# Attention's scores as split products, with the remainder of the keys as two row tiles

## The chip, the cores and the metric

The kernel runs on one core of a Trainium2 chip. The metric is the device time of one execution in microseconds (us), lower is better. The engines of the core run their own instruction streams in order and wait for one another by semaphores: TensorE (matmuls, and transposes as matmuls), VectorE (DVE in the rows), ScalarE (ACT), GpSimd (POOL), and SyncE (SP), whose queue issues most transfers (DMA).

## The reference

A model of two blocks works on 1024 tokens of width 1024 in float32. The first block has two layers; each mixes three branches, of which only the second one matters here: differential attention with 4 heads. Queries and keys of a head have two components of 64 features each, with rotary positions; values have 128 features.

```
q, k: (2 components, 4 heads, 1024 tokens, 64)       # after rope, q scaled by 1/8
for each block of 128 queries:
    s = einsum('cbhqd,cbhkd->cbhqk', qblk, k)         # both components
    p = softmax(s, axis=-1)
    w = p[0] - lam * p[1]
    o = einsum('bhqk,bhkv->bhqv', w, v)
o = rms_norm(o) * (1 - lambda_init);  output o * silu(g)
```

The other branches (gated linear scans), the output projection, and the second block (convolution, recurrent unit, 32 routed experts) are the rest of the time and are not edited.

## The kernel before, in words

Matmuls that need float32 accuracy are done in one of two ways. The projections split each operand into a float32r part and the float32r rest (`ATh` and `ATl` hold the normalized input so, features over partitions) and add three float32r products (`mm3`, L379 to L381). Attention's products are plain fp32 matmuls, which the hardware runs as two records for each instruction.

In each layer the projections of heads 0 and 1 (`dq0`, `dk0`, `dv0`) come first, among the scans. `rope` (L913 to L928) rotates a pair of 128-token tiles with VectorE and GpSimd, transposes them with TensorE into PSUM (`pT`), evacuates them with ScalarE (L925) into a tile `h` and stores it to the DRAM buffers `qd` and `kd` (L928). `values` (L933) stores v into `dvd`. Then comes the attention proper. Head 0 runs while the projections of heads 2 and 3 (`other_projections`: 24 steps, five behind each of the first periods) are still going; heads 1 to 3 run without them.

A head needs Q, K and v in SBUF. `head_prep` makes the list of its loads (L982 to L984). For head 0 they go to tiles of the pool `hp_` (`QS`, `KH`, `v`). For heads 1 to 3 they go into regions of `ATh` and `ATl`, the normalized input itself, so they must wait until the last projection has read that region: heads 1 and 3 take feature slices 6 and 7, head 2 takes slices 2 and 3. Both components lie side by side in the free dimension; the 64 features take 64 partitions. Q is loaded twice, into partitions 0 to 63 and 64 to 127; K's first 512 keys go to the lower partitions, the second 512 to the upper ones.

The work of attention is written as periods, one for each block of 128 queries, 8 for each head. A period does two half steps, one for each component. In a half step TensorE does the scores of the new block (`scores`, L1002: two matmuls of 64 rows, one for each half of the keys, on row tiles that lie side by side, into two PSUM banks `pS`), four transposes of the weights of a block two periods older (`turned`, L1034, `pW`), and two products with v of one still older (`weighted`, L1049, `pO`). VectorE takes the row maximum (L1005), ScalarE the exponential (L1007), VectorE joins the components (L1019 to L1022). Every four blocks `squared`, `summed` and `headnorm` (L1058 to L1072) normalize. `put` chains these calls on TensorE, VectorE and ScalarE, so their order on each of the engines is the written one. Everything else is placed by a planner that works from modelled times when the program is built: it picks what it takes for ready, in the order of the program's text. So a transfer that stands later in the text can be issued ahead of one that is not ready.

From `PRELOAD`, a head's loads are listed during the head before it (block 5 of head 0, block 2 of heads 1 and 2), three for each period. PSUM has two buffers for `pS`, three for `pW` and the projections, one for `pO`.

Of the kernel before, what the change touches and what calls it, by code (L numbers as in the profile page):

```python
# [11 lines left out]
F32 = mybir.dt.float32  # L12
# [215 lines left out]
def r32(ap):  # L228
    return ap.bitcast(F32)
# [7 lines left out]
def kernel(ctx: ExitStack, tc: tile.TileContext, A: dict, out: bass.AP, upto=99, dbg=None):  # L237
# [41 lines left out]

    qd = dr.tile([4, 64, 2, S], F32, name="qd")  # L280
    kd = dr.tile([4, 64, 2, S], F32, name="kd")
    dvd = dr.tile([4, 128, S], F32, name="dvd")
# [446 lines left out]
    for l in range(DEPTH):  # L729
# [170 lines left out]
        def place(at, shape, dt, **kw):  # L900
            if at[1] in ("st", "sh"):
                kw["bufs"] = 2
            return at[0].tile(shape, dt, tag=at[1], name="pl", **kw)

        def rope(n, hp, i, w, acc, tr, at, eng=G):
# [14 lines left out]
            for hh in range(2):  # L920
                for ii in range(2):
                    T.transpose(pT[:, hh, ii * 128:ii * 128 + 128],
                                asm[0][:, ii, hh * 4:hh * 4 + 4].rearrange("p b d -> p (b d)"), ident)
            h = place(at[2], [128, 2, 256], F32)
            rope.last = SC.activation(h, pT, AF.Copy, scale=0.125 if n == 0 else 1.0)  # L925
            dst = (qd, kd)[n][2 * hp:2 * hp + 2, :, :, (i - 1) * 128:(i + 1) * 128]
            for c in range(2):
                SY.dma_start(dst[:, :, c].rearrange("h x t -> x h t"), h[c * 64:c * 64 + 64])  # L928

# [6 lines left out]

        at1 = ((st, "q"), (st, "t2r"), (st, "sgb"))
        for n, nm in enumerate(("dq", "dk")):
# [27 lines left out]
        def head_prep(h):  # L966


            if h == 0:
                Q, K, v = (hp_.tile([128, n, 512], F32, tag=t, name=t) for t, n in (("QS", 4), ("KH", 2), ("v", 2)))  # L970
            else:
                a = 2 if h == 2 else 6
                Q, K, v = r32(ATh[:, a:a + 2]), r32(ATl[:, a]), r32(ATl[:, a + 1])
            if h == 0:
                Q = Q.rearrange("p (c k) t -> p c (k t)", c=2)
                v = v.rearrange("p k t -> p (k t)")
            else:
                K = K.rearrange("p (c t) -> p c t", c=2)
            loads = []
            for d_ in range(2):  # L980
                rows = slice(d_ * 64, d_ * 64 + 64)
                loads.append(lambda rows=rows: SY.dma_start(Q[rows], qd[h]))  # L982
                loads.append(lambda rows=rows, d_=d_: SY.dma_start(K[rows], kd[h, :, :, d_ * 512:d_ * 512 + 512]))
            loads.append(lambda: SY.dma_start(v, dvd[h]))  # L984
            return {"h": h, "ops": (Q, K, v.rearrange("p (k d) -> p k d", k=8)), "loads": loads}

# [8 lines left out]
        def scores(q, c):  # L995

            st, i, sm = q["st"], q["i"], q["sm"]
            Q, K = st["ops"][:2]
            p = sc_.tile([128, 2, 512], F32, tag="s", name="pS")
            for kc in range(2):  # L1000
                rows = slice(kc * 64, kc * 64 + 64)
                put("pe", lambda: T.matmul(p[:, kc, :], Q[rows, c, i * 128:(i + 1) * 128], K[rows, c, :],  # L1002
                                           start=True, stop=True))
            pf = p.rearrange("p a b -> p (a b)")
            put("dve", lambda: V.tensor_reduce(sm[:, c:c + 1], pf, axis=AX.X, op=OP.max, negate=True))  # L1005
            ec = aw.tile([128, S], F32, tag=f"e{c}", name=f"e{c}", bufs=3)
            put("act", lambda: SC.activation(ec, pf, AF.Exp, bias=sm[:, c:c + 1], accum_out=sm[:, 2 + c:3 + c]))  # L1007
            q["e"].append(ec)
# [90 lines left out]
        def other_projections():  # L1099
            got = {0: wq1}  # L1100
            at2 = ((hp_, "st"), (aw, "sg"), (hp_, "sh"))

# [1025 lines left out]
```

## Time and profile before

| | |
|---|---|
| median of 3 runs | 2889.11 us (2883.72 to 2891.49) |
| the profiled execution's own time | 2893.09 us |
| its span, first to last instruction | 2891.2 us |
| TensorE busy with matmuls | 2669.6 us (92%) |
| VectorE, ScalarE busy | 1712.3 us (59%), 1262.3 us (44%) |
| mean granted TensorE clock | 0.966 |

Busy shares are means over stages with different limits. The records of a matmul overlap their neighbours, so the time of a group on TensorE is best read from the start of one group to the start of the next. The granted clock is the share of full speed; it has two levels, 1.00 and 0.50.

### The profile page before, as it was taken

To read this page: it belongs to the slowest core of one execution; us is meant where nothing else is said; L and a number is where in the kernel's file an instruction comes from. 1 tells how busy PE (TensorE), PEld (TensorE's weight loads), DVE (VectorE), ACT (ScalarE), POOL (GpSimd) and SP (SyncE) were. 2 spreads that over 40 slices of the span, in tenths; PEclk is the share of its full clock that TensorE was granted. 3 is DMA by queue.
4 is the path that set the end of the run, shared out by engine and by line. 5 is a ranking of instruction groups with operands and counts; after the bars stand their busy time and mean duration, and the time that the engine had idled before them with its cause. 6 is when DMAs were issued, how large, how long until landed. Compare 5 with 4: busy or idle time off the path is not lost. (4 is left out here: it accounts for less than half of the span.)

```text
span 2891.2 us, 39821 instructions
## 1 busy us (share of the span) xinstructions
PE 2669.6 (92%) x15462; PEld 2087.7 (72%) x15462; DVE 1712.3 (59%) x2530; ACT 1262.3 (44%) x2078; POOL 722.4 (25%) x564
## 2 busy tenths in 40 slices
PE   7998998999999999989999999889799999999968
PEld 6887887755988878878558887679566666566558
DVE  6767663476357576633773493663655456455566
ACT  5343322366343424323663412642554445455545
POOL 1323131142214141311431342530211111121122
PEclk9999999999999999999999999989899999999979
DMA  4221223432322212233413323033688889799761
GB/s 152 66 79 62 88 88 79 102 102 63 128 85 73 79 64 94 83 80 81 111 63 132 109 75 106 30 119 124 272 338 344 328 306 392 298 360 377 312 265 71
DMA packets 140213, 446.78 MB, mean 155 GB/s; under 512 B 14432, under 2 KB 51360, under 8 KB 113760
## 3 DMA queue, kind: packets, MB, share of 16 engines
q1 hardware_dynamic: 131040, 412.26, 40.5%
q0 software_dynamic: 8960, 31.72, 3.1%
q8 instruction: 128, 2.10, 0.3%
q14 instruction: 85, 0.70, 0.1%
HBM read 367.25 MB, written 76.68 MB: 154 GB/s over the span
## 5 line engine op out<-in xcount | busy, mean ns | idle before, releaser
L379 PE MATMUL pK<-wh,ATh 128*128 128x256 f32 x1280 | 373.8, 293 | 24.3 <-DVEq L623 10.7
L1650 DVE TENSOR_TENSOR ews<-raw,ews 128x2048 fp32r<-128x2048 f32 x120 | 277.3, 2325 | 187.6 <-ACT ews L1649 185.8
L380 PE MATMUL pK<-wl,ATh 128*128 128x256 f32 x1280 | 370.5, 290 | 7.3 <-DVE wl L362 7.3
L381 PE MATMUL pK<-wh,ATl 128*128 128x256 f32 x1280 | 366.7, 288 | 1.8 <-POOL ATl L1414 1.8
L379 PE MATMUL pF<-ATh,wh 128*128 128x512 f32 (+1 forms) x800 | 321.4, 403 | 1.7 <-ACT g L1335 0.9
L380 PE MATMUL pF<-ATl,wh 128*128 128x512 f32 (+1 forms) x800 | 320.9, 401 | 0.3 <-DVE ATl L350 0.2
L381 PE MATMUL pF<-ATh,wl 128*128 128x512 f32 (+1 forms) x800 | 319.5, 400 | 0.1
L1649 ACT ACTIVATE ews<-raw 128x2048 fp32r<-128x2048 f32 x124 | 234.6, 1910 | 156.5 <-PE h L381 62.6
L379 PEld LDWEIGHTS pK<-wh,ATh 128*128 128x128 f32 x1280 | 249.2, 195 | 38.8 <-issue 16.1
L380 PEld LDWEIGHTS pK<-wl,ATh 128*128 128x128 f32 x1280 | 249.5, 195 | 14.3 <-DVE wl L362 8.1
L381 PEld LDWEIGHTS pK<-wh,ATl 128*128 128x128 f32 x1280 | 247.9, 194 | 5.5 <-issue 2.8
L1005 DVE TENSOR_REDUCE sm<-pS 128x1 f32<-128x1024 f32 x128 | 156.3, 1221 | 111.2 <-PE pS L1002 111.1
L1007 ACT ACTIVATE e<-pS,sm 128x1024 f32<-128x1024 f32 x128 | 142.4, 1113 | 170.3 <-DVE sm L1005 164.6
L379 PEld LDWEIGHTS pF<-ATh,wh 128*128 128x128 f32 (+1 forms) x800 | 150.1, 188 | 40.3 <-issue 4.0
L380 PEld LDWEIGHTS pF<-ATl,wh 128*128 128x128 f32 (+1 forms) x800 | 149.8, 187 | 38.4 <-issue 5.6
L379 PE MATMUL h<-ews,xh 128*128 128x512 f32 (+1 forms) x416 | 168.6, 410 | 9.3 <-ACT xh L1831 5.1
L381 PEld LDWEIGHTS pF<-ATh,wl 128*128 128x128 f32 (+1 forms) x800 | 149.9, 187 | 36.9 <-issue 4.3
L380 PE MATMUL h<-ews,xh 128*128 128x512 f32 (+1 forms) x416 | 168.5, 406 | 2.8 <-DVE ews L1650 2.8
L381 PE MATMUL h<-ews,xl 128*128 128x512 f32 (+1 forms) x416 | 168.0, 405 | 3.4 <-DVE xl L1833 3.4
L1848 POOL DMA_INDIRECT xb<-hfd,tab x38 | 53.2, 1399 | 456.1 <-PE pT L1830 447.6
L379 PE MATMUL pK<-wo,ATh 128*128 128x256 f32 x512 | 149.0, 291 | 9.7 <-ACT ATh L1195 9.7
L380 PE MATMUL pK<-wo,ATh 128*128 128x256 f32 x512 | 147.2, 288 | 0.0
(462 smaller groups left out, 6086.5 us busy)
## 6 DMA issues: line engine op xcount, KB each, us to landing
raw<-in_w_dram SPq DMA_DIRECT2D x192, 1024.0 KB, 11.1
ws<-in_wp_dram SPq DMA_DIRECT2D x64, 512.0 KB, 4.8
xd<-x SPq DMA_DIRECT2D x24, 512.0 KB, 2.6
x<-xd SPq DMA_DIRECT2D x17, 512.0 KB, 6.0
x<-in_x_dram SPq DMA_DIRECT2D x16, 512.0 KB
sgd<-sgb SPq DMA_DIRECT2D x32, 256.0 KB, 2.8
sg<-sgd SPq DMA_DIRECT2D x32, 256.0 KB
yd<-oT SPq DMA_DIRECT2D x32, 256.0 KB, 2.0
```

Source lines behind the costliest of these rows:

```text
L379: T.matmul(ps, ah, bh, start=first, stop=False)
L380: T.matmul(ps, ah, bl, start=False, stop=False)
L381: T.matmul(ps, al, bh, start=False, stop=last)
L1005: put("dve", lambda: V.tensor_reduce(sm[:, c:c + 1], pf, axis=AX.X, op=OP.max, negate=True))
L1007: put("act", lambda: SC.activation(ec, pf, AF.Exp, bias=sm[:, c:c + 1], accum_out=sm[:, 2 + c:3 + c]))
L1649: SC.activation(w[:, 0], s_, AF.Copy)
L1650: eng.tensor_tensor(w[:, 1], s_, r32(w[:, 0]), op=OP.subtract)
L1848: G.indirect_dma_start(out=xb[:n], out_offset=None, in_=hfd, in_offset=bass.IndirectOffsetOnAxis(ap=idx, axis=0))
```

## The change

`rope` now writes two tiles: `h`, the transposed tile rounded to float32r by ScalarE as before, and `lo`, the rest, which VectorE computes from `pT` and `h`; both are stored, so `qd` and `kd` get a dimension for the two parts. `lo` has one buffer.

The scores become three products: with Q the two parts of the queries, one below the other over 128 partitions, and K the keys' first part, twice, once below the other, one float32r matmul of 128 rows gives (first + rest of q) x (first part of k) for each half of the keys. Then a pair of 64-row matmuls adds the first part of q (Q2) times the rest of k (Kl). The product of the two rests is left out, as in the projections.

A head's loads go from 5 to 8: Q over all 128 partitions in one transfer, K twice with all 1024 keys, Q2 twice, Kl in two halves, v. Heads 1 and 3 now take slices 4 to 7 of `ATh` and `ATl`, head 2 slices 0 to 3.

```diff
-    qd = dr.tile([4, 64, 2, S], F32, name="qd")
-    kd = dr.tile([4, 64, 2, S], F32, name="kd")
+    qd = dr.tile([4, 2, 64, 2, S], F32, name="qd")
+    kd = dr.tile([4, 2, 64, 2, S], F32, name="kd")
...
-            h = place(at[2], [128, 2, 256], F32)
-            rope.last = SC.activation(h, pT, AF.Copy, scale=0.125 if n == 0 else 1.0)
-            dst = (qd, kd)[n][2 * hp:2 * hp + 2, :, :, (i - 1) * 128:(i + 1) * 128]
-            for c in range(2):
-                SY.dma_start(dst[:, :, c].rearrange("h x t -> x h t"), h[c * 64:c * 64 + 64])
+            h = place(at[2], [128, 2, 256], F32R)
+            lo = place(at[3], [128, 2, 256], F32R, bufs=at[3][2])
+            sc = 0.125 if n == 0 else 1.0
+            rope.last = SC.activation(h, pT, AF.Copy, scale=sc)
+            V.scalar_tensor_tensor(lo, pT, sc, r32(h), op0=OP.mult, op1=OP.subtract)
+            dst = (qd, kd)[n][2 * hp:2 * hp + 2, :, :, :, (i - 1) * 128:(i + 1) * 128]
+            for a, t in enumerate((h, lo)):
+                for c in range(2):
+                    SY.dma_start(dst[:, a, :, c].rearrange("h x t -> x h t"), r32(t[c * 64:c * 64 + 64]))
...
-                a = 2 if h == 2 else 6
-                Q, K, v = r32(ATh[:, a:a + 2]), r32(ATl[:, a]), r32(ATl[:, a + 1])
...
-            for d_ in range(2):
-                rows = slice(d_ * 64, d_ * 64 + 64)
-                loads.append(lambda rows=rows: SY.dma_start(Q[rows], qd[h]))
-                loads.append(lambda rows=rows, d_=d_: SY.dma_start(K[rows], kd[h, :, :, d_ * 512:d_ * 512 + 512]))
+                a = 0 if h == 2 else 4
+                Q, Q2, K = ATh[:, a:a + 2], ATh[:, a + 2:a + 4], ATl[:, a:a + 2]
+                Kl, v = ATl[:, a + 2].rearrange("p (c t) -> p c t", c=2), ATl[:, a + 3]
+            v = r32(v)
+            loads = [lambda: SY.dma_start(r32(Q), qd[h].rearrange("a x c t -> (a x) c t"))]
+            halves = [(slice(d_ * 64, d_ * 64 + 64), slice(d_ * 512, d_ * 512 + 512)) for d_ in range(2)]
+            for rows, t in halves:
+                loads.append(lambda rows=rows: SY.dma_start(r32(K[rows]), kd[h, 0]))
+            for rows, t in halves:
+                loads.append(lambda rows=rows: SY.dma_start(r32(Q2[rows]), qd[h, 0]))
+                loads.append(lambda rows=rows, t=t: SY.dma_start(r32(Kl[rows]), kd[h, 1, :, :, t]))
             loads.append(lambda: SY.dma_start(v, dvd[h]))
...
+            for kc in range(2):
+                put("pe", lambda: T.matmul(p[:, kc, :], Q[:, c, t], K[:, c, kc * 512:kc * 512 + 512],
+                                           start=True, stop=False))
             for kc in range(2):
                 rows = slice(kc * 64, kc * 64 + 64)
-                put("pe", lambda: T.matmul(p[:, kc, :], Q[rows, c, i * 128:(i + 1) * 128], K[rows, c, :],
-                                           start=True, stop=True))
+                put("pe", lambda: T.matmul(p[:, kc, :], Q2[rows, c, t], Kl[rows, c, :], start=False, stop=True))
```

## Rows read from the trace of the kernel before

**Rows 1.** The page's engine totals: busy us, share of the span, instructions.
```profile
PE 2669.6 (92%) x15462; PEld 2087.7 (72%) x15462; DVE 1712.3 (59%) x2530; ACT 1262.3 (44%) x2078; POOL 722.4 (25%) x564
```

**Rows 2.** Windows by stage: stretch, length, busy us of each engine, clock, DMA.
```profile
455.00:571.00 116.00, 110.20 (x753) 91.20 (x753) 49.07 (x82) 35.10 (x61) 17.46 (x32) 0.96 0.37 89
571.00:712.00 141.00, 130.63 (x602) 70.62 (x602) 106.33 (x148) 93.88 (x169) 57.41 (x53) 1.00 0.29 84
```

**Rows 3.** Timeline of TensorE in head 1: start, us, what, records.
```profile
606.27 1.13 PE L1002 MATMUL pS<-ATl,ATh 64*128 64x512 f32 x4
607.33 0.66 PE L1034 MATMUL pW<-ident,e 128*128 128x128 f32 x4
607.82 1.03 PE L1049 MATMUL pO<-wT,ATl 128*128 128x256 f32 x4
608.78 1.13 PE L1002 MATMUL pS<-ATl,ATh 64*128 64x512 f32 x4
```

**Rows 4.** Timeline of TensorE, the half step that waits.
```profile
616.32 1.13 PE L1002 MATMUL pS<-ATl,ATh 64*128 64x512 f32 x4
...
619.53 1.13 PE L1049 MATMUL pO<-wT,ATl 128*128 128x256 f32 x4 [1.50 <-DVE oT L1059]
620.60 1.13 PE L1002 MATMUL pS<-ATl,ATh 64*128 64x512 f32 x4
```

**Rows 5.** Timeline of VectorE around it.
```profile
612.54 1.23 DVE L1005 TENSOR_REDUCE sm<-pS 128x1 f32<-128x1024 f32 x1 [0.68 <-PE pS L1002]
...
616.46 0.42 DVE L1129 CAST wo<-wos 128x512 fp32r<-128x512 f32 x1
618.79 0.69 DVE L1059 TENSOR_TENSOR oT<-pO,sg 128x512 f32<-128x512 f32 x1 [1.91 <-ACT sq L1058]
```

**Rows 6.** Timeline of SP's queue at head 0's start, layer 0.
```profile
459.39 0.51 SPq L982 DMA_DIRECT2D QS<-qd  x1
...
461.87 0.59 SPq L984 DMA_DIRECT2D v<-dvd  x1
```

**Rows 7.** Timeline of TensorE there.
```profile
461.12 0.28 PE L379 MATMUL pK<-wh,ATh 128*128 128x256 f32 x1
465.60 2.04 PE L1002 MATMUL pS<-KH,QS 64*128 64x512 f32 x2 [4.20 <-DMA KH<-kd]
...
469.57 3.37 PE L1002 MATMUL pS<-KH,QS 64*128 64x512 f32 x6
```

**Rows 8.** Window behind that wait (columns as rows 2).
```profile
465.60:472.40 6.80, 6.80 (x16) 3.42 (x16) 0.72 (x1) 0.00 (x0) 0.00 (x0) 0.50 0.59 142
```

**Rows 9.** Timeline of TensorE at head 1's start.
```profile
570.95 1.12 PE L1002 MATMUL pS<-ATl,ATh 64*128 64x512 f32 x2
...
572.40 1.09 PE L1002 MATMUL pS<-ATl,ATh 64*128 64x512 f32 x2 [0.33 <-DMA ATl<-kd]
...
573.42 0.66 PE L1034 MATMUL pW<-ident,e 128*128 128x128 f32 x4
```

**Rows 10.** Window of float32r products of 512 columns alone (tile pF).
```profile
1650.00:1700.00 50.00, 50.00 (x223) 41.42 (x222) 0.00 (x0) 5.21 (x9) 1.00 0.13 43
```

**Rows 11.** Transfers from 460.5 to 469.8 us, head 0's loads.
```profile
DMA packets 592, 2.10 MB, mean 226 GB/s; under 512 B 80, under 2 KB 80, under 8 KB 464
```

**Rows 12.** Transfers from 2140 to 2160 us, experts' weights of 1024 KB each.
```profile
DMA packets 1305, 8.44 MB, mean 422 GB/s; under 512 B 148, under 2 KB 148, under 8 KB 404
```

**Rows 13.** Timeline of SP's queue before head 1.
```profile
555.39 0.55 SPq L983 DMA_DIRECT2D ATl<-kd  x1
556.03 1.83 SPq L982 DMA_DIRECT2D ATh<-qd  x3
...
559.77 0.68 SPq L983 DMA_DIRECT2D ATl<-kd  x1
```

**Rows 14.** A group of the page's kind: the nearest VectorE row to the added operation.
```profile
L350 DVE TENSOR_TENSOR ATl<-pT,ATh 128x512 fp32r<-128x512 f32 x64 | 43.6, 688 | 24.6 <-ACT ATh L349 24.1
```

More of the change, by code (lines that the diff above doesn't have):

```diff
@@ L935, in values @@
                          h.rearrange("p (h c) -> p h c", h=2))
-        at1 = ((st, "q"), (st, "t2r"), (st, "sgb"))
+        at1 = ((st, "q"), (st, "t2r"), (st, "sgb"), (st, "lo", 1))
         for n, nm in enumerate(("dq", "dk")):
@@ L969, in head_prep @@
             if h == 0:
-                Q, K, v = (hp_.tile([128, n, 512], F32, tag=t, name=t) for t, n in (("QS", 4), ("KH", 2), ("v", 2)))
-            else:
-                a = 2 if h == 2 else 6
-                Q, K, v = r32(ATh[:, a:a + 2]), r32(ATl[:, a]), r32(ATl[:, a + 1])
[L974 to L979, printed above, removed]
-            for d_ in range(2):
-                rows = slice(d_ * 64, d_ * 64 + 64)
-                loads.append(lambda rows=rows: SY.dma_start(Q[rows], qd[h]))
-                loads.append(lambda rows=rows, d_=d_: SY.dma_start(K[rows], kd[h, :, :, d_ * 512:d_ * 512 + 512]))
+                Q, Q2, K, v = (hp_.tile([128, 4, 512], F32R, tag=t, name=t) for t in ("QS", "KH", "KL", "v"))
+                Q, Q2, K = (t.rearrange("p (c k) t -> p c (k t)", c=2) for t in (Q, Q2, K))
+                Kl, v = v[:, 0:2], v[:, 2:4].rearrange("p k t -> p (k t)")
+            else:
+                a = 0 if h == 2 else 4
[9 more added lines that the diff above has]
+                loads.append(lambda rows=rows, t=t: SY.dma_start(r32(Kl[rows]), kd[h, 1, :, :, t]))
             loads.append(lambda: SY.dma_start(v, dvd[h]))
-            return {"h": h, "ops": (Q, K, v.rearrange("p (k d) -> p k d", k=8)), "loads": loads}
+            return {"h": h, "ops": (Q, K, v.rearrange("p (k d) -> p k d", k=8), Q2, Kl), "loads": loads}
         turn = {}
@@ L997, in scores @@
             st, i, sm = q["st"], q["i"], q["sm"]
-            Q, K = st["ops"][:2]
+            Q, K, _, Q2, Kl = st["ops"]
             p = sc_.tile([128, 2, 512], F32, tag="s", name="pS")
+            t = slice(i * 128, (i + 1) * 128)
+            for kc in range(2):
+                put("pe", lambda: T.matmul(p[:, kc, :], Q[:, c, t], K[:, c, kc * 512:kc * 512 + 512],
+                                           start=True, stop=False))
             for kc in range(2):
                 rows = slice(kc * 64, kc * 64 + 64)
-                put("pe", lambda: T.matmul(p[:, kc, :], Q[rows, c, i * 128:(i + 1) * 128], K[rows, c, :],
-                                           start=True, stop=True))
+                put("pe", lambda: T.matmul(p[:, kc, :], Q2[rows, c, t], Kl[rows, c, :], start=False, stop=True))
             pf = p.rearrange("p a b -> p (a b)")
@@ L1100, in other_projections @@
             got = {0: wq1}
-            at2 = ((hp_, "st"), (aw, "sg"), (hp_, "sh"))
+            at2 = ((hp_, "st"), (aw, "sg"), (hp_, "sh"), (aw, "lo", 1))
             def step(n, i):
```

## The prediction

> **What bounds the kernel now.** I read the engine totals first: TensorE is busy for 92% of the span, VectorE for 59% [rows 1]. The change touches attention, once in each layer, so I then read those stages. In layer 0 the stretch from 455 to 571 us runs head 0's attention together with the second half of the projections, and 571 to 712 us runs heads 1 to 3 alone [rows 2]. TensorE is busy 95% and 93% there, VectorE 42% and 75%. Layer 1 repeats both stretches.
>
> The timeline of heads 1 to 3 shows the beat [rows 3]. A half step (one component of one block of 128 queries) takes 2.51 us from one score product to the next: 1.06 us for the scores (pS), 0.49 us for four transposes (pW), 0.96 us for two products with v (pO). TensorE goes from one to the next without a wait, so it sets the pace. Once in eight half steps it doesn't: pO waits until oT has been read, and the half step takes 4.28 us (616.32 to 620.60) [rows 4]. That wait ends a chain of VectorE and ScalarE work that begins with an earlier score [rows 5]; only what is in front of the chain's first score can shorten the block. VectorE's work of a full step lies between 612.54 and 616.88, 4.34 us against 5.02 us for TensorE.
>
> Two places are slower than this beat, the starts of head 0 and of head 1. At head 0's start the loads of Q, K and v are issued from 459.39 to 461.87 us [rows 6], and TensorE runs out of projection work at 461.4 us, idles 4.20 us for K, and begins the second half of its first scores only at 469.57 us [rows 7]. The granted clock is 0.50 for the 6.8 us behind that wait, the lower of the two levels (1.2 instead of 2.4 GHz) [rows 8]. At head 1's start the second pair of scores waits too: it begins at 572.40 us where the first began at 570.95, and the transposes follow at 573.42 instead of 572.01 (570.95 and the usual 1.06), 1.4 us lost [rows 9].
>
> **What the change does, part by part.**
>
> *Scores.* Before, a score pair is two fp32 products of 64 rows by 512 columns, four passes (x4) in 1.06 us [rows 3]. pO's fp32 passes, at half the columns, show what a pass costs: four of 256 columns in 0.96 us with the change of tile behind them, so about 0.43 us for 512 columns. Four in a row would need 1.7 us; so two run side by side, 2 x 0.43 = 0.86 us, and 0.20 us goes to changing the tile and the exposed weight load. After, there are two full-height float32r products and then a pair of 64 rows. A float32r product of 512 columns takes 50 us / 223 = 0.224 us [rows 10]. If the pair runs side by side, as the fp32 pair does, pS is 3 x 0.224 + 0.20 = 0.87 us, 0.19 us less. If it does not, it is 4 x 0.224 + 0.20 = 1.10 us, 0.04 us more. No row has a float32r product on 64 rows; the nearest is the fp32 pair on the very same tiles, so I take side by side. There are 128 half steps (2 layers, 4 heads, 8 blocks, 2 components); in one of eight the chain hides it: 112 x 0.19 = **21 us gained** (bounds: 5 lost, 24 gained).
>
> *Bytes to load.* A head's loads were Q 2 x 512 KB, K 2 x 256 KB and v 512 KB. They become Q 1 MB in one transfer over 128 partitions, K 2 x 512 KB, Q2 2 x 512 KB, Kl 2 x 256 KB, v 512 KB: twice the bytes, and all but v are needed for the first scores to end. The loads of 64 partitions each, with both halves outstanding, come at 226 GB/s, in a stretch whose queue is full [rows 11]; 1 MB loads over 128 partitions come at 422 GB/s elsewhere [rows 12]. So before, Q and K are 1.57 MB / 226 = 7.0 us; after, Q is 1.05 MB / 422 = 2.5 us, the rest 2.62 MB / 226 = 11.6 us, together 14.1 us.
>
> The Trainium skill has this on its page "SBUF — State Buffer", section "Door 1: The DMA port swizzle (why [64,N] ≈ [32,N])": a transfer over 64 partitions reaches half the ports, and its table has 196 GB/s for 64 partitions and 328 for 128, at 1 MiB. The trace shows the same halving, at higher rates (226 and 422). By the page's rates Q and the rest would be an estimated 3.2 + 13.4 = 16.6 us, and each start would come some 2 to 4 us later than I say below; the measured rates decide.
>
> *Head 0's start.* Before, the second half of the first scores began 10.2 us after the first issue (459.39 to 469.57) for 7.0 us of moving, 3.2 us on top [rows 6, 7]. After: 14.1 + 3.2 = 17.3 us, 7.1 us later. TensorE doesn't lose all of it, since projection products stand between; their place is fixed by the planner, which will put more of them ahead when it expects more loads. Between nothing covered and all, I take 4.6 us as covered, because there is projection work in plenty; that leaves 2.5 us lost and 1 us more at the low clock: 3.5 us a layer, **7 us** (bounds: 0, and 7.1 + 3.4 = 10.5 us a layer).
>
> *Head 1's start.* This is the place that I fear most. Its loads overwrite the normalized input, so they can only go when the last projection has read it: the first of them is the last of three Q loads issued up to 557.9 us [rows 13], and head 1's scores begin at 570.95 us [rows 9], 13 us later. Three of head 2's loads are issued in front of them, because the part of the buffer that head 2 takes is read earlier: of the first K load and the next three Q loads, two Q and the K are head 2's [rows 13]. Ahead of head 1's last load were 0.26 + 1.05 + 1.57 MB and a 0.13 MB store, 3.0 MB / 226 = 13.3 us; it was waited for until 572.40, 17.0 us after the first issue, so 3.7 us on top [rows 9, 13]. After, head 2's part begins at the very first slice, and two of its loads (Q, one K: 2.5 + 2.3 us) fit before head 1's first may go. With the store and head 1's 14.1 us that is 19.5 + 3.7 = 23.2 us from about 555.0 (a step before 555.39), so 578.2 us. TensorE wants them at about 570.4 (five shorter scores, then two full products): 7.8 us of waiting, 6.4 us more than now. A wait of 4.20 us had the clock halved for 6.8 us, 3.4 us of work [rows 8]; I add 2.5 us: 8.9 us a layer, **18 us** (bounds: head 1 first, 7.8 - 4.8 = 3.0 us, 1.6 us a layer over now; three of head 2's first, 12.1 us a layer). Nothing else is there for TensorE, as its attention calls are in a fixed order. Heads 2 and 3 have 47 us each to load in (141 us for three heads [rows 2]).
>
> *The rests.* 32 more VectorE operations on a transposed tile, 0.69 us each by the nearest row (22 us) [rows 14], and 64 more stores. They lie beside projections where VectorE is at 42% [rows 2], but the PSUM buffer is held 0.7 us longer and "lo" has one buffer: **1 us** (bounds 0 and 6).
>
> *Sum.* -21 + 7 + 18 + 1 = +5 us on the profiled execution's own 2893.09 us (span 2891.2, the rest around it): 2898 us. The median of the runs is 4.0 us under that execution, so 2894 us.
>
> **The rivals.** *The loads are hidden (faster).* If the planner lets head 1's loads go first and fills head 0's start, the extra waits fall to 3 and 2 us and the sum is -21 + 3 + 2 + 1 = -15 us: 2874 us. It decides at some 5 us of waiting a layer, head 0's and head 1's together. For it: the planner already put projection products between the halves of the first scores. Against: it let three of head 2's loads pass, and TensorE idled at both starts. *The pair is not side by side (slower).* Then the products cost 5 us instead of giving 21: +31 us, 2920 us. Against it stands the fp32 pair's 1.06 us. *The softmax becomes the pace.* VectorE's 4.34 us a step leaves 0.3 us of a shortened 4.64; if its waits eat half of the gain, the sum is +15 us, 2904 us. For it speaks the block that already ends in VectorE and ScalarE [rows 4, 5].
>
> **How the numbers follow.** A change under 0.3% (8.7 us) can't be told from none. My case (the loads' waits give back the products' gain) has 0.55, and its own range is -6 to +20 us, 2883 to 2909; of it 0.05 falls to faster, 0.30 to no change, 0.20 to slower. Loads hidden: 0.23, of it 0.20 faster, 0.03 the same. Pair not side by side: 0.14, slower. Softmax: 0.08, of it 0.06 slower. That makes 0.25, 0.35 and 0.40. The range reaches from 2874 us to 2917 us, to the edge of either side's rival.
>
> **What would show it.** In the changed profile a regular half step of heads 1 to 3 should be 2.32 us instead of 2.51, with the last two of the four score products starting together; 2.55 us means not side by side, and about 2.4 us with waits on sm or e means the softmax. The first scores of head 1 should wait for Kl or Q2 until about 578 us with the lower clock behind it; a wait under 3 us there, in both layers, makes me wrong towards faster. Head 0's first scores should be complete some 7 us later after the first load's issue. The prediction falls, too, if the planner moves work outside the attention by more than a few us.

## The result, and the profile after

The changed kernel takes 2912.89 us (median of 8 runs, 2903.61 to 2919.98), the kernel before 2888.82 us (8 runs, 2883.39 to 2893.80). The ratio is 1.0083, 95% interval 1.0071 to 1.0096: slower by 24 us, which is more than the 0.3% that can be told from no change. The forecast was 2894 us, with a range of 2874 to 2917 us and slower as the likeliest sign. So the sign and the range held, and the middle missed by 19 us, which is most of the change. The profiled execution has a span of 2911.4 us, 20.2 us over the span before.

The engine totals hardly move; they answer to [rows 1], and the reader can see only that TensorE is as busy as it was:

```profile
PE 2666.7 (92%) x15462; PEld 2130.3 (73%) x15462; DVE 1727.0 (59%) x2562; ACT 1261.0 (43%) x2078; POOL 720.2 (25%) x564
```

To see where 20 us went I cut the span into stages at three kinds of marks that every version has: the issue of head 0's first load, the start of the first exponential of head 1, and the start of the last exponential of head 3 (ScalarE's `e<-pS`, in the timeline). The stage "loads to head 1" holds head 0's attention and both starts; "heads 1 to 3" is TensorE's own stretch; "elsewhere" is all that lies outside the two. The last has no work that the products or the loads touch, apart from the rests' operations in layer 0's and layer 1's first projections.

| us, both layers | before | after | difference |
|---|---|---|---|
| loads to head 1 | 115.8 + 114.8 = 230.6 | 121.2 + 121.5 = 242.7 | +12.1 |
| heads 1 to 3 | 132.2 + 132.2 = 264.5 | 137.9 + 142.3 = 280.2 | +15.7 |
| elsewhere | 2396.1 | 2388.4 | -7.7 |
| span | 2891.2 | 2911.4 | +20.2 |

These are one execution of each kernel; the one of the kernel before, at 2893.09 us, lies 4.3 us over its median.

**The beat.** This is the timeline of TensorE in head 1, which answers to [rows 3]. From score product to score product it is 2.35 us where it was 2.51. The two 64-row products (L1013) take 0.50 us together, and one alone takes 0.50 us in the view of this tile (median 500 ns): they run side by side. Inside the half step the time does not fall where it did: from the scores' start to the transposes' is 1.17 us now (614.16 to 615.33, before 1.06), and from pO's start to the next scores' 0.68 us (615.83 to 616.51, before 0.96). The records overlap, so only the whole half step is safely compared.

```profile
613.48 1.03 PE L1059 MATMUL pO<-wT,ATl 128*128 128x256 f32 x4
614.16 0.81 PE L1009 MATMUL pS<-ATl,ATh 128*128 128x512 f32 x2
614.90 0.50 PE L1013 MATMUL pS<-ATl,ATh 64*128 64x512 f32 x2
615.33 0.66 PE L1044 MATMUL pW<-ident,e 128*128 128x128 f32 x4
615.83 1.03 PE L1059 MATMUL pO<-wT,ATl 128*128 128x256 f32 x4
616.51 0.81 PE L1009 MATMUL pS<-ATl,ATh 128*128 128x512 f32 x2
```

**Head 0's start** [rows 6, 7]. SP's queue and TensorE, layer 0. The first scores begin 11.1 us after the first issue (458.12 to 469.23) where it was 6.2, and the last pair's first product waits for Kl until 472.93. Its second waits until 476.47 us, 18.35 us after the first issue, where the first scores' second half began 10.2 us after it. TensorE fills that time with projections: it idles 3.7 us for loads here (3.0 in layer 1), where it idled 4.2 (3.8). The rows:

```profile
458.12 0.34 SPq L984 DMA_DIRECT2D QS<-qd  x1
...
462.42 0.62 SPq L991 DMA_DIRECT2D v<-dvd  x1
```

```profile
469.23 0.72 PE L1009 MATMUL pS<-KL,QS 128*128 128x512 f32 x2 [1.87 <-DMA KL<-kd]
...
472.93 0.46 PE L1013 MATMUL pS<-v,KH 64*128 64x512 f32 x1 [0.98 <-DMA v<-kd]
```

**Head 1's start** [rows 9, 13]. In SP's queue the first Q (552.33) and the first K (begun at 552.84) are head 2's; head 1's loads follow from 554.59. TensorE waits three times, 7.9 us in all, and the transposes come 8.64 us after the first scores, where it was 2.47 (layer 0):

```profile
552.33 0.42 SPq L984 DMA_DIRECT2D ATh<-qd  x1
552.84 1.66 SPq L987 DMA_DIRECT2D ATl<-kd  x1
554.59 0.54 SPq L984 DMA_DIRECT2D ATh<-qd  x1
...
561.24 0.54 SPq L990 DMA_DIRECT2D ATl<-kd  x1
```

```profile
569.26 0.69 PE L1009 MATMUL pS<-ATl,ATh 128*128 128x512 f32 x2 [1.40 <-DMA ATl<-kd]
572.86 0.76 PE L1013 MATMUL pS<-ATl,ATh 64*128 64x512 f32 x1 [2.91 <-DMA ATl<-kd]
577.21 0.76 PE L1013 MATMUL pS<-ATl,ATh 64*128 64x512 f32 x1 [3.59 <-DMA ATl<-kd]
577.90 1.12 PE L1044 MATMUL pW<-ident,e 128*128 128x128 f32 x4
```

**Heads 1 to 3.** Windows of layer 0 (columns as [rows 2], whose second row has a clock of 1.00 for the whole stretch). The first is the stretch behind the wait at head 1's start. Each of the others is eight half steps, from one exponential to the eighth behind it, and is called a block from here on; before, a block took 22.7 us:

```profile
571.00:581.20 10.20, 4.75 (x12) 3.17 (x12) 2.85 (x5) 1.70 (x3) 1.15 (x2) 0.50 1.05 228
...
602.70:625.90 23.20, 21.37 (x102) 14.35 (x100) 17.81 (x26) 15.04 (x27) 10.96 (x10) 0.94 0.39 115
625.90:654.50 28.60, 24.64 (x100) 16.03 (x100) 18.76 (x27) 15.05 (x27) 10.70 (x10) 0.83 0.73 180
654.50:676.20 21.70, 19.87 (x100) 13.47 (x99) 16.73 (x24) 15.04 (x27) 6.96 (x7) 1.00 0.13 41
```

A block of 21.7 us at a clock of 1.00 gains 1.0 us. Seven half steps shorter by the forecast's 0.19 us would be 1.3 us; they are shorter by 0.16 us, and the eighth, which waits for oT, is longer by as much (4.44 us, 671.51 to 675.95, where it was 4.28). And only some blocks have even this gain. A block of 23.2 us has a stretch at 0.50, the lower of the two levels (1.2 instead of 2.4 GHz), behind the wait for oT; such a fall costs 23.24 - 21.72 = 1.5 us. And one block in each layer takes 28.6 or 31.1 us. TensorE's timeline at an oT wait answers to [rows 4], where the idle time is 1.50 us and the clock stays up; the window behind it shows the fall:

```profile
601.62 1.99 PE L1059 MATMUL pO<-wT,ATl 128*128 128x256 f32 x4 [1.83 <-DVE oT L1069]
```

```profile
601.70:605.10 3.40, 3.40 (x8) 1.96 (x8) 2.57 (x4) 1.69 (x3) 1.04 (x2) 0.51 0.45 136
```

The long block is a new wait. SP's queue has seven of head 3's eight loads from 619.70 to 623.35 us, and a load of the output weights, wos, behind them at 624.04. VectorE takes its instructions in order: its cast of wos stands in front of a maximum of the scores (L1015) and waits 4.81 us; ScalarE's exponential waits for that maximum, and TensorE for the exponential's buffer. The load of wos lands at 640.02 us, 16 us after its issue:

```profile
619.70 0.33 SPq L984 DMA_DIRECT2D ATh<-qd  x1
...
624.04 0.57 SPq L1136 DMA_DIRECT2D wos<-in_wo_dram  x1
```

```profile
640.05 0.43 DVE L1139 CAST wo<-wos 128x512 fp32r<-128x512 f32 x1 [4.81 <-DMA wos<-in_wo_dram]
640.39 1.22 DVE L1015 TENSOR_REDUCE sm<-pS 128x1 f32<-128x1024 f32 x1
```

```profile
642.90 1.22 PE L1009 MATMUL pS<-ATl,ATh 128*128 128x512 f32 x2 [2.81 <-ACT e L1017]
```

### The profile page after: what moved, and what is told of

Same layout as the page of the kernel before. It is cut to its first block, busy times and chain, and to the rows that moved or that the text cites. A ratio compares the mean times of both kernels' runs of the same rounds, so it can differ in the third digit from the quotient of the medians.

```text
span 2911.4 us, 40006 instructions
## 1 busy us (share of the span) xinstructions
PE 2666.7 (92%) x15462; PEld 2130.3 (73%) x15462; DVE 1727.0 (59%) x2562; ACT 1261.0 (43%) x2078; POOL 720.2 (25%) x564
## 5 line engine op out<-in xcount | busy, mean ns | idle before, releaser
L379 PEld LDWEIGHTS pK<-wh,ATh 128*128 128x128 f32 x1280 | 249.1, 195 | 38.5 <-issue 21.5
L380 PEld LDWEIGHTS pK<-wl,ATh 128*128 128x128 f32 x1280 | 249.1, 195 | 14.2 <-DVE wl L362 8.1
L1015 DVE TENSOR_REDUCE sm<-pS 128x1 f32<-128x1024 f32 x128 | 156.3, 1221 | 105.3 <-PE pS L1013 102.7
```

The source lines that it names most:

```text
L379: T.matmul(ps, ah, bh, start=first, stop=False)
L380: T.matmul(ps, ah, bl, start=False, stop=False)
```

## The experiments

Twelve kernels ran. My theory after the result: the loads' bytes and their places in SP's queue cost what the products gain, and the queue behind head 3's loads and the falls of the clock come on top. The rivals were that the loads are free, that the products themselves are slower, and that the difference lies outside attention. The stages of each run stand here once, as sums over both layers, from one profiled execution each; "ratio" is time against the kernel before in runs beside it, with its 95% interval.

| kernel | median us | ratio | loads to head 1 | heads 1 to 3 | elsewhere |
|---|---|---|---|---|---|
| before | 2888.8 | 1 | 230.6 | 264.5 | 2396.1 |
| after | 2912.9 | 1.0083 (1.0071 to 1.0096) | 242.7 | 280.2 | 2388.4 |
| e1 old products | 2903.0 | 1.0061 (1.0045 to 1.0078) | 249.1 | 267.2 | 2379.4 |
| e2 no rest loads | 2873.1 | 0.9956 (0.9941 to 0.9972) | 225.4 | 263.3 | 2378.6 |
| e3 wide loads | 3200.8 | 1.1100 (1.1079 to 1.1121) | 431.2 | 377.5 | 2389.1 |
| e4 head 1 first | 2880.3 | 0.9970 (0.9958 to 0.9982) | 233.7 | 277.1 | 2374.1 |
| e5 plain wide loads | 2861.6 | 0.9924 (0.9902 to 0.9946) | 217.5 | 261.6 | 2381.4 |
| e6 wos elsewhere | 2873.5 | 0.9957 (0.9943 to 0.9970) | 227.1 | 267.6 | 2378.0 |
| e7 filler | 2876.2 | 0.9966 (0.9952 to 0.9980) | 229.5 | 267.0 | 2382.5 |
| e8 two pO | 2918.0 | 1.0103 (1.0071 to 1.0134) | 255.4 | 274.9 | 2389.0 |
| e9 wide and filler | 2857.3 | 0.9901 (0.9872 to 0.9930) | 217.6 | 252.5 | 2382.5 |
| e10 rests only | 2873.7 | 0.9946 (0.9926 to 0.9966) | 226.2 | 264.5 | 2381.8 |
| e11 rests unstored | 2877.6 | 0.9956 (0.9939 to 0.9973) | 226.6 | 264.5 | 2379.4 |
| e12 no lo op | 2895.3 | 1.0022 (1.0009 to 1.0035) | 242.1 | 274.5 | 2376.0 |

The last column is to be read first. It varies from 2374 to 2396 us although most edits touch nothing there, and before is its highest value. Part of that is the spread of executions, which lie 5 to 17 us apart for one kernel. A median over the whole kernel therefore says little about an edit worth 5 us; the two middle columns say more, though the stage from the loads to head 1 moves too, by 4 us in e10, whose loads and score products have before's number and shape.

**e1, the old products with the new loads.**

```diff
-                put("pe", lambda: T.matmul(p[:, kc, :], Q[:, c, t], K[:, c, kc * 512:kc * 512 + 512],
-                                           start=True, stop=False))
...
-                put("pe", lambda: T.matmul(p[:, kc, :], Q2[rows, c, t], Kl[rows, c, :], start=False, stop=True))
+                put("pe", lambda: T.matmul(p[:, kc, :], r32(Q2[rows, c, t]),
+                                           r32(K[rows, c, kc * 512:kc * 512 + 512]), start=True, stop=True))
```

> The new loads and layout stay; the scores are one fp32 pair again (64 rows, both score tiles side by side), taken from the queries' and the keys' first parts, so the rests are loaded but left out of the products. Theory (the loads and what queues behind them cost, the products gain): a half step is 2.51 us again, head 0's and head 1's starts are late as in the changed kernel, and the wait for wos in heads 2 and 3 stays; with about 9 us for head 0's starts, 12 to 15 for head 1's and 6 for wos that is some 2889 + 28 = 2917 us. The granted clock stays 1.00 in the normalization blocks without a load's wait. Rival 1 (the loads are free, the products cost the time): 2889 us. Rival 2 (the clock falls in these blocks because the loads' transfers run beside them, not because of the products): about 2920 us, and the clock falls to 0.50 in the same blocks.

2903 us, with 249.1 us from the loads to head 1: the new loads alone cost 18.5 us there against before. So rival 1 (the loads are free) falls. Windows of heads 1 to 3, layer 0, second block and the last two and a half: 22.7 us and a clock of 1.00 as before. So rival 2 falls: the transfers run beside these blocks here too, and the clock does not fall.

```profile
604.20:626.90 22.70, 21.20 (x100) 11.37 (x100) 17.75 (x25) 15.01 (x28) 11.10 (x10) 1.00 0.41 101
...
649.60:713.70 64.10, 61.09 (x287) 33.19 (x286) 49.09 (x66) 42.92 (x78) 22.80 (x22) 1.00 0.17 55
```

One part of my theory missed: there is no wait for wos here. Kl has no reader in this kernel, so four loads and not seven of head 3's stand together in front of wos. The time is 14 us under the 2917 us of that theory; the missing wait is some 6 of them, and elsewhere is 16.7 us shorter than before, for which it had no term.

**e2, the new products without the rests' loads.**

```diff
-            for rows, t in halves:
-                loads.append(lambda rows=rows: SY.dma_start(r32(Q2[rows]), qd[h, 0]))
-                loads.append(lambda rows=rows, t=t: SY.dma_start(r32(Kl[rows]), kd[h, 1, :, :, t]))
...
-                put("pe", lambda: T.matmul(p[:, kc, :], Q2[rows, c, t], Kl[rows, c, :], start=False, stop=True))
+                put("pe", lambda: T.matmul(p[:, kc, :], Q[rows, c, t], K[rows, c, kc * 512:kc * 512 + 512],
+                                           start=False, stop=True))
```

> The products keep their number, shapes and order, but Q2 and Kl are not loaded: the last pair reads the same rows of Q and K instead, so the rests are left out of the result's sum in their proper form. 2.6 MB are loaded for a head instead of 4.2. Theory: head 0's start costs at most 1 us more than before, the wait at head 1's start falls under 2 us, and wos is no longer late; that takes 9 + 12 + 6 us off 2913, some 2886 us, with the clock's falls in the normalization blocks still there; 2871 us if these go too. Rival 1 (the loads are free): 2913 us. A half step stays 2.35 us by either.

2873 us, 13 us under the 2886 that my theory had for falls that stay; 9.8 us of the difference to the changed kernel lie elsewhere. From the loads to head 1 it is 17.3 us less than in the changed kernel, and 5.2 us less than before. TensorE's wait for a load at head 1's start is 0.8 us (layer 0), and no long block is left. The falls stay, in five of the six blocks of layer 0 (23.2 to 23.3 us instead of 21.7, the short last one 19.2 instead of 17.7), but in two of the six of layer 1, behind the same waits of 1.83 us. With e1 that ties them to the products and not to the loads; why some waits pass without a fall stays open.

**e3, the same bytes in three transfers over 128 partitions.**

```diff
...
+            k0, q0, k1 = kd[h, 0], qd[h, 0], kd[h, 1]
+            dup = [[0, 2], [2 * S, 64], [S, 2], [1, S]]
+            loads.append(lambda: SY.dma_start(r32(K), bass.AP(tensor=k0.tensor, offset=k0.offset, ap=dup)))
+            loads.append(lambda: SY.dma_start(r32(Q2), bass.AP(tensor=q0.tensor, offset=q0.offset, ap=dup)))
+            loads.append(lambda: SY.dma_start(r32(Kl), bass.AP(tensor=k1.tensor, offset=k1.offset,
+                                                               ap=[[512, 2], [2 * S, 64], [S, 2], [1, 512]])))
```

> The same 4.2 MB a head, but K, Q2 and Kl each in one transfer over 128 partitions instead of two over 64 (the source is read twice by a stride of nothing). Theory: all of it comes at the 422 GB/s of the 128 partition rows, 9.9 us a head instead of some 16. Head 1's last wanted load lands about 5 us earlier in each layer, head 0's start loses 2 to 3 us less, head 3's loads are through before wos is wanted: about 2913 - 10 - 5 - 8 = 2890 us, and the unknown is what the shorter waits give back of the clock. Rival (the pace of these loads is set by the bytes or the source's reads, not by the partitions): they take 16 us still, 2913 us. The clock's falls in the blocks that wait for no load should stay by my theory.

3201 us, and both theories are wrong. The transfers from 464 to 500 us move at 54 GB/s, and the queue keeps SP busy for 18.6 us with one issue:

```profile
DMA  1111111111111111111111111111111111111111
GB/s 55 64 55 55 55 55 55 55 55 55 55 55 55 55 55 55 55 46 55 46 55 55 55 55 55 55 55 55 55 55 55 36 46 55 55 55 55 55 55 55
DMA packets 237, 1.93 MB, mean 54 GB/s; under 512 B 2, under 2 KB 2, under 8 KB 2
```

```profile
460.56 18.59 SPq L990 DMA_DIRECT2D v<-kd  x1
```

The queue's packets took 12.6% of the time of 16 DMA engines in that stretch, about two engines' worth. All three sources begin with a dimension of two. That this dimension is what spreads a transfer over the engines fits these numbers and was only argued; e5 moves the same tiles with plain sources and does not show it.

**e4, head 1's loads in front.** The parts of the overwritten buffers change places:

```diff
-                a = 0 if h == 2 else 4
+                a = 4 if h == 2 else 0
```

> Heads 1 and 3 take the part of the overwritten buffers that head 2 had (the normalized input's first four slices), and head 2 takes the other; nothing else changes. Theory: the part that is read earlier is free earlier, so head 1's loads stand in front of all of head 2's; the 4.8 us of head 2's Q and K are no longer ahead, head 1's wait falls from some 9 us to 3 to 4 us a layer, and its half clock shortens: about 2913 - 12 = 2901 us. Rival (the queue's order comes from the planner and not from when the part is read, or the whole buffer comes free at once): head 2's two loads stay in front, 2913 us.

2880 us. All of head 1's loads now stand in front of head 2's. In heads 1 to 3's stretch of layer 0 TensorE waits 3.3 us for head 1's loads, where the changed kernel waits 7.9; the wait behind wos (ACT e) stays, at 4.7 us against 2.8:

```profile
PE pO L1059 <- DVE oT L1069: 8.9, 5, 1.8
PE pS L1009 <- ACT e L1017: 4.7, 1, 4.7
PE pS L1013 <- DMA ATl<-kd: 3.3, 2, 3.0
```

The two stages of attention are 12.1 us shorter than in the changed kernel, which is what I expected (12). The other 14 us between the two profiled executions lie elsewhere, where the edit changes only the order of the work (more on this behind e12). The runs from here to e9 stand on e4.

**e5, plain wide loads.** Q's first part is stored three times, K's twice, and the keys' rests in two row blocks, so that each of Q, K, Q2 and Kl is one plain load:

```diff
-            for a, t in enumerate((h, lo)):
-                for c in range(2):
-                    SY.dma_start(dst[:, a, :, c].rearrange("h x t -> x h t"), r32(t[c * 64:c * 64 + 64]))
...
+            copies = 3 if n == 0 else 2
+            for c in range(2):
+                part = slice(c * 64, c * 64 + 64)
+                for hh in range(2):
+                    SY.dma_start((qd, kd)[n][2 * hp + hh, 0:copies, :, c, b].rearrange("a x t -> x a t"),
+                                 r32(h[part, hh]).unsqueeze(1).to_broadcast([64, copies, 256]))
+                to = qd[two, 3, :, c, b] if n == 0 else kl[two, (i - 1) // 4, :, c, g]
+                SY.dma_start(to.rearrange("h x t -> x h t"), r32(lo[part]))
...
+            loads = [lambda t=t, d=d: SY.dma_start(r32(t), d.rearrange("a x c t -> (a x) c t"))
+                     for t, d in ((Q, qd[h, 2:4]), (K, kd[h]), (Q2, qd[h, 0:2]), (Kl, kl[h]))]
```

> On top of head 1's loads in front: the first parts of Q are stored three times and those of K twice, the keys' rests in two row blocks, so that Q, K, Q2 and Kl of a head are each one plain load over 128 partitions. Theory: 4.2 MB at the 422 GB/s of such rows are 9.9 us instead of some 16. Head 1's wait of 3 us goes, head 0's first scores come some 4 us sooner, and wos, behind head 3's loads, is no longer late (4.7 us and the half clock behind it): 2880 - 3 x 2 - 4 x 2 - 6 x 2 = 2854 us. Rival 1 (it is the number of transfers and the source's reads that count, not the partitions): 2880 us. Rival 2 (the added store traffic fills the queue beside the projections): the head 0 stretch grows by what the loads give, 2880 to 2890 us.

2862 us. Head 0's loads move at 403 GB/s from 460 to 470 us, where the changed kernel's loads over 64 partitions come at 213 GB/s from 464.5 to 474.5 us:

```profile
DMA packets 673, 4.03 MB, mean 403 GB/s; under 512 B 63, under 2 KB 63, under 8 KB 300
```

```profile
DMA packets 529, 2.13 MB, mean 213 GB/s; under 512 B 83, under 2 KB 83, under 8 KB 340
```

In heads 1 to 3 of layer 0 TensorE waits for no load and for no exponential any more. Against e4 the two stages fall by 31.7 us, more than the 26 I expected, and elsewhere gives 7.3 us back. The Trainium skill, page "SBUF — State Buffer", section "Door 1: The DMA port swizzle (why [64,N] ≈ [32,N])", says that a transfer over 64 partitions reaches half the ports; the two rows above agree, at 213 against 403 GB/s.

**e6, wos on GpSimd's queue.**

```diff
-                SY.dma_start(s_, A["wo"][l][cc][:, i * 2:i * 2 + 2])
+                G.dma_start(s_, A["wo"][l][cc][:, i * 2:i * 2 + 2])
```

> On top of head 1's loads in front: the wos loads are issued by GpSimd, on its own queue, so they no longer stand behind head 3's loads. Theory (VectorE waits in order for wos, ScalarE's exponential and TensorE behind it): the half step of 7.4 us in layer 0 and of 7.6 us in layer 1 goes back to 4.4 us, and the lower clock behind it with it; 5 us a layer, 2880 - 10 = 2870 us. Rival 1 (wos is late because the DMA engines are full of head 3's bytes, whichever queue it stands in): the wait stays, 2880 us. Rival 2 (GpSimd's order holds its other work back while it waits to issue): 2885 us or more.

2873 us, 0.0013 of the ratio under e4, where the intervals overlap. The stage tells it: heads 1 to 3 take 267.6 us, 9.5 us less than in e4, VectorE waits for wos not at all in layer 0 and 1.5 us in layer 1, and no block is above 24.4 us. So the place in the queue did it, and not the engines being full.

**e7, added products where TensorE waits for oT.**

```diff
+            if st["h"] and i % 4 == 0 and c == 0:
+                for kc in (0, 1, 0, 1):
+                    put("pe", lambda: T.matmul(p[:, kc, :], Q[:, c, t], K[:, c, kc * 512:kc * 512 + 512],
+                                               start=True, stop=True))
```

> On top of head 1's loads in front: four added float32r products (0.9 us, overwritten by the real ones) in the half step in which TensorE waits for oT, heads 1 to 3. They lie ahead of the wait and don't stand before the chain that ends it. Theory (the granted clock falls after TensorE has stood idle for 1.8 us and more at the oT wait): the idle time shrinks to about 1 us, the falls to 0.50 go away, and each is worth some 1.5 us: about 8 falls, 2880 - 12 = 2868 us. Rival 1 (the falls come from the sort of products, not from the wait): they stay, 2880 us. Rival 2 (the added products delay the scores that begin the next chain): 0.9 us for each of 12 blocks, 2891 us.

The idle time in front of pO falls from 1.83 to 0.92 us, and the clock behind it stays at 1.00 (timeline of TensorE, and the window behind the wait):

```profile
618.06 1.13 PE L1063 MATMUL pO<-wT,ATl 128*128 128x256 f32 x4 [0.92 <-DVE oT L1073]
```

```profile
618.10:621.50 3.40, 3.40 (x17) 2.59 (x18) 3.33 (x5) 1.69 (x3) 1.08 (x2) 1.00 1.07 229
```

Every block that waits for no load takes 21.7 us, in both layers: the falls are gone, and the added products cost nothing in these blocks. The edit does two things at once, more work in front of the wait and less idle time in it; which of them holds the clock up isn't told apart. Heads 1 to 3 are 10.1 us shorter than in e4. Over the whole kernel it can't be told from e4 (2876 and 2880 us, overlapping intervals): elsewhere was 8.4 us longer in the profiled execution.

**e8, two buffers for pO.**

```diff
-        tp = p2.enter_context(tc.tile_pool(name=f"at{l}", bufs=3, space=PSUM))
-        op_ = p2.enter_context(tc.tile_pool(name=f"ao{l}", bufs=1, space=PSUM))
+        tp = p2.enter_context(tc.tile_pool(name=f"at{l}", bufs=2, space=PSUM))
+        op_ = p2.enter_context(tc.tile_pool(name=f"ao{l}", bufs=2, space=PSUM))
```

> On top of head 1's loads in front: two buffers for pO and two instead of three for the transposes and projections of the attention stage (the banks are all taken). Theory (what is left at each fourth block of queries is the wait of pO for oT, and the clock falls behind it): the 4.44 us half step becomes 2.35 us and the lower clock behind it goes too; 14 such places at 2.1 us and 8 falls at 1.5 us, 2880 - 40 = 2840 us. Rival 1 (the softmax's chain is the bound of these eight half steps, so the wait only moves to another buffer): heads 1 to 3 stay as they are, 2880 us. Rival 2 (with two buffers the transposes wait for ScalarE's copies in every half step, and head 0's projections too): slower, 2900 us or more.

2918 us. The wait for oT is gone, but a block at a clock of 1.00 takes 22.7 us, 1.0 us more than with the wait: TensorE waits for other buffers instead, as both rivals had it. Head 0, whose projections share the two banks, takes the rest (255.4 against 233.7 us). The waits of TensorE from 590 to 730 us:

```profile
PE pS L1009 <- ACT e L1017: 5.7, 6, 1.3
PE pW L1044 <- ACT wT L1046: 5.4, 7, 0.8
PE pN L1075 <- ACT wT L1046: 3.7, 5, 0.8
```

**e9, e5 with e7's products.**

> The loads over 128 partitions with head 1's in front, and the four added products in the half step of the oT wait. Theory: the two act on different things, so the six falls of the clock that are left with the wide loads go, 1.5 us each: 2861 - 9 = 2852 us, every block of heads 1 to 3 at 4.44 and 2.34 us. Rival (the falls that are left with the wide loads come from something that the added products don't reach): 2861 us.

2857 us, the fastest here: 1.0% under before and the lowest in heads 1 to 3. All ten full blocks take 21.7 us at a clock of 1.00; three rows of layer 0:

```profile
569.70:591.40 21.70, 20.78 (x104) 14.21 (x103) 17.39 (x25) 15.04 (x27) 9.71 (x9) 1.00 0.36 124
591.40:613.10 21.70, 20.78 (x104) 14.23 (x103) 17.74 (x27) 15.04 (x27) 10.98 (x10) 1.00 0.41 135
613.10:634.80 21.70, 20.77 (x104) 14.22 (x103) 17.73 (x27) 15.04 (x27) 10.99 (x10) 1.00 0.64 221
```

This is the clean size of the products' gain: 126.2 us for heads 1 to 3 in each layer against 132.2, so 6.0 us a layer. Its interval overlaps e5's, so by the median alone the step from e5 to e9 isn't told apart; by the stage it is 9.1 us.

**e10 and e11, the rests alone, on the kernel before.** e10 computes and stores them, e11 only computes them. The loads, and the score products in number and shape, are before's.

```diff
+            lo = place(at[3], [128, 2, 256], F32R, bufs=at[3][2])
...
+            V.scalar_tensor_tensor(lo, pT, sc, r32(h), op0=OP.mult, op1=OP.subtract)
...
+            for a, t in enumerate((h, lo)):
```

> The kernel before with one part of the change alone: the rests are computed on VectorE and stored (32 operations, 64 stores more), but neither loaded nor used, so the scores are made of the first parts only. The prediction's term for this is 1 us, 0 to 6 slower: 2889 + 1 = 2890 us. Theory now: the stage from the output projection to layer 1's head 0, which the changed kernel runs 5 us faster after its late start is given back, is faster here too, since the planner orders the projections with the added operations in another way: 2884 us. Rival (these 5 us come from the changed loads or from the new products): 2890 us.

> The kernel before with the rests computed on VectorE and nothing else: they are neither stored nor used. The run with the stores too was 13 us faster than before where 1 us slower was predicted. Theory: the 32 operations on VectorE (and the buffer that they hold) change the order in which the planner puts the products of the other stages, and that is what is gained: about 2874 us. Rival (the stores change it): 2888 us.

Added work makes the kernel faster: 2873.7 us against 2886.4 us beside it (13 us), and 2877.6 against 2889.0 us (11 us) without the stores. Heads 1 to 3 are as before to 0.1 us, at 22.7 us a block. In the profiled executions 4 us lie between the loads and head 1, and the rest elsewhere: from layer 0's last exponential to layer 1's first load 557.5 us became 550.0 and 549.3 us, and from layer 1's last exponential to the end, where no rests are computed, 1379.2 us became 1371.9 and 1370.9 us. The stores are not needed for it.

**e12, the changed kernel without the rests' operation.**

```diff
-            lo = place(at[3], [128, 2, 256], F32R, bufs=at[3][2])
...
-            V.scalar_tensor_tensor(lo, pT, sc, r32(h), op0=OP.mult, op1=OP.subtract)
...
-            for a, t in enumerate((h, lo)):
+            for a, t in enumerate((h, h)):
```

> The changed kernel with the rests left out of the computation: the first part is stored in both places, so loads, stores and products are all there and the 32 operations on VectorE and their buffer are not. Theory (these operations make the planner's order better by 13 us): without them the changed kernel is slower still, about 2926 us. Rival (the stores do, or the order is already another in the changed kernel): 2913 us, or 2912 for the work taken off VectorE.

2895 us, 0.6% under the changed kernel by the two ratios. My theory said 2926 us, and it falls: taking the operation away helps as adding it did. Of the 18.7 us between the two profiled executions 12.4 us lie elsewhere and 5.7 us in heads 1 to 3 (the long block of layer 1 is 26.0 us instead of 31.1). So it is not the operation. What differs is the order of the instructions. In the last stretch, behind layer 1's attention, TensorE's matmuls stand in one and the same order in e1, e10 and e11, and the stretch takes 1370.4 to 1371.9 us; before and the changed kernel share another order for the last 4447 of its 6658 matmuls, and take 1379.2 and 1378.5 us. A part of it is a single wait of TensorE in the second block, for a gather of rows (`xb`). It is over 10 us in before, the changed kernel and e8, and 3 to 7 us in all the others (5.8 us in e10, 3.1 in e4; the rows are before's, the changed kernel's and e12's):

```profile
PE pT L1830 <- DMA xb<-hfd,tab: 10.4, 1, 10.4
PE pT L1840 <- DMA xb<-hfd,tab: 10.6, 1, 10.6
PE pT L1838 <- DMA xb<-hfd,tab: 4.0, 1, 4.0
```

So some 10 us of this kernel go with the order, by these single executions. No run changes the order alone, and what in it does this stays open.

## Why the prediction was right, and where it wasn't

Its frame held: the products gain, the two starts give it back. In the terms of the sum, from the stage table and the blocks (21.72 us clean, 22.72 us before):

- **Scores, 21 us gained forecast; about 17 measured.** Side by side was right, the half step is 2.35 us where 2.32 was forecast. 0.16 us for each of head 0's 32 half steps are an estimated 5.1 us, and e9 shows 12.0 us for heads 1 to 3. The term was a little large: the half step that waits does not stay as it was, it grows by 0.16 us. The 0.87 us for pS alone can't be read in the rows, where the time shows at the step from pO to the scores.
- **The two starts, 7 + 18 = 25 us forecast; 21 to 25 measured.** The stage from the loads to head 1 grew by 12.1 us; the 5.1 us that its products gain are to be added, and 3.8 us that the first block of head 1 takes over 21.72 us (23.39 and 23.87 us), with the clock at 0.50 to 581.2 us: 21.0 us against before. Against e10, whose order has nearly as many projection products in that stretch as the changed kernel's (572 and 570 against 572 and 569; before 557), the stage grew by 16.5 us, and the starts are 25.4 us. Head 1's start is 19 us of it by either, for 18 forecast; head 0's is 2 or 6.4 us, for 7. e1, with the loads and without the products, has 18.5 us in the stage and 2.8 us in the first blocks. The wait was forecast until 578.2 us and the last Kl product began at 577.21; two of head 2's loads stood in front, as the prediction had it, and e4 shows that their place matters. The rate for 64 partitions was read a little high: in the 2.10 MB of [rows 11] moves v, which is over 128 partitions, so its 226 GB/s is a mean of both; the changed kernel's loads show 213.
- **"Heads 2 and 3 have 47 us each to load in" is the step that failed.** Heads 2 and 3 themselves are in time, but what stands behind their loads in the same queue is not. The blocks of 28.58 and 31.07 us are 16.2 us over 21.72, both layers. e6 moved wos to another queue, and the wait went (but for 1.5 us on VectorE in layer 1). Each of the two blocks has a fall of the next item in it as well, behind the oT waits at 624.86 and 1436.53 us, so the wait for wos itself is some 13 us.
- **Not in the sum: the falls of the clock behind the oT wait.** Outside of the long blocks they add 7.6 us: five stretches at about 1.5 us (23.24 instead of 21.72), two of them in the last, shorter block; with the two in the long blocks some 10.6 us. The prediction took the clock's fall as something that follows a long wait for a load alone. e1 (old products, no falls), e2 (new products without the loads, falls) and e7 (idle time filled, no falls) put them on the shorter products with the longer idle time in front of pO.
- **The rests, 1 us slower forecast; nothing of the kind measured.** The operation takes 687 ns as forecast, but e10 and e11 are faster by 13 and 11 us and e12, without it, by 18 us. The prediction's own remark, that it falls if other work is moved by more than a few us, is what happened: elsewhere is 7.7 us shorter.

Against before these are -17.1 + 21.0 + 16.2 + 7.6 - 7.7 = +20.0 us, against +20.2 in the spans. They must close, since they are cut from the stages; what the experiments add is whose each term is. So the middle of the forecast missed by two terms that were left out, 23.8 us, of which the work elsewhere took a third back in this execution. That the time stayed inside the range is in part luck: without those 7.7 us, which no term had, it would have been some 2920 us.

Of the rivals, the pair that is not side by side is refuted by the 0.50 us. That the loads are hidden came for head 0 in part, where projections fill the time, and not for head 1; e5 and e9 bring it about by other means. The softmax as the pace did not come: with the clock up the blocks are 21.7 us; e8 shows that without the wait for oT other buffers hold the same eight half steps.

## What to carry to other kernels

A product that gets cheaper by taking more bytes has to be priced at every start at which its operands are fresh, and then at every transfer that stands behind those bytes in the same queue, whoever wants it: an engine that takes its work in order passes such a wait on to all that follows. Bytes that had to be written to 64 partitions twice were better stored twice and loaded once over 128 here. And when an edit to a kernel with a planned order moves the time by half a per cent, compare the stages that it touches before putting the total down to the edit, in either sense.

## What the runs showed of the hardware that I had not expected

- With shorter products in front of the same kind of wait, and a longer idle time in it, the granted clock fell. Before, TensorE stood idle 1.50 us at pO and the clock stayed at 1.00; after, it stood idle 1.83 us and the clock went to 0.50 for 3.4 us behind it, seven times of eight and not always (behind the same 1.83 us at 675.17 us it stayed at 1.00). With 0.92 us of idle time it stayed up in all of them. Added products that nobody reads so made heads 1 to 3 faster by 10.1 us (e7 against e4) and 9.1 us (e9 against e5).
- A load whose source begins with a dimension of two moved at 54 GB/s and held SP's queue for 18.6 us with one issue (e3), where a plain load into the same tiles moved at 403 GB/s (e5).
